# A hybrid sparse-attention block on one core: the softmax gate as a per-partition scalar, and the relu of the index scores left in PSUM

## The chip, the core and the metric

The kernel runs on 1 core of one Trainium2 chip. The metric is the device time of one execution in microseconds (us); before the change the median of 3 runs is 802.14 us (801.01 to 804.88). Lower is better.

## What is computed

One decoder block for 512 tokens of width 1024, in float32: a pre-norm, one wide input projection, two attention branches (A and B), sigmoid gates that merge them, an output projection, and a squared-relu MLP. The change touches two places, which the reference states so:

```python
# branch A: an index score picks 128 of the 512 keys for each query
s_h = jnp.einsum('bqhd,bsd->bqhs', qi, k_i).astype(jnp.float32)      # 8 index heads
score = jnp.einsum('bqh,bqhs->bqs', wi, jax.nn.relu(s_h))            # weighted sum of relus
...
# branch B: softmax over the selected keys (s), over a window (w) and over compressed keys (c)
gates = jax.nn.sigmoid(gates.astype(jnp.float32)).reshape(B, S, 3, G, R)
o = (gb[:, :, 0, :, :, None] * o_c + gb[:, :, 1, :, :, None] * o_s
     + gb[:, :, 2, :, :, None] * o_w)
```

A softmax row is `e / sum(e)`; the gate of a query and a head is one number per query, so the kernel multiplies it into `1 / sum(e)` before that factor is applied to the row.

## The kernel before

Tokens lie on the 128 partitions in four blocks j = 0 to 3, and all matmuls of weight and activation are split into a high and a low part, which makes three matmuls of one. The program has these stages: norm and first projections (to about 75 us), the attention stage (75 to about 375 us), the merge and output projection, the MLP (from about 460 us).

The attention stage is a list of 96 **units**, one per head, kind (`s` and `w` of branch B, then `a` of branch A) and block j. Unit j works on 128 queries and n = 128(j+1) keys. The 64 units of branch B come first (75 to about 290 us). A unit goes through `logits` (PE, into a PSUM tile of the tag `lg`, two buffers), `biased` (DVE, line 944: adds the bias strip, gives the negated logits `nl` and the row's minimum `nm`), `exps` (ACT, line 951: `pb` and the row sum `sm`), `recip` (DVE, lines 955 and 957), `norm` (ACT, line 964: `pb` times the factor `r`), `transposes` (PE, line 969) and `store` (ACT line 976, DVE line 977). The loop at line 1210 writes out the steps of three neighbouring units interleaved, and between them it takes matmuls from a list of other work ("filler": the remaining projections and the attention-times-value products) at a set pace. The order on PE is fixed by this loop; the order on DVE and ACT is made by a scheduler from the same program.

Beside the units run the **index scores** (`scores_job`, line 623) of the blocks j = 1, 2, 3. For each index head (for j = 1: for two heads at a time) PE writes the scores `sc` into a tile of the same tag `lg` (line 656), ACT takes the relu (line 647) into an SBUF tile `rl` of the tag `pb`, which has three buffers and is also that of `exps`, and DVE adds the relu times the head's weight `wi` to `work` in SBUF (line 651). The step of a head's relu and sum comes one step ahead of the next head's matmul, and in between the loop issues a unit's logits, so that the two buffers of `lg` go alternately to logits and to scores. There are 20 such relus and 24 sums. After them follow 16 rounds of max and match-replace per block (lines 669 and 670) on DVE.

POOL works at the same time, for the most part on the low parts of the weights: line 107 subtracts 128x1024 of SBUF from 128x1024 of SBUF.

The gate is a column of the SBUF tile `gates`, of 128x1; `r` and `sm` are SBUF tiles of 128x1 too:

```python
            self.r = r = t2.tile([P, 1], F32, tag="r", bufs=4, name="r" + self.name)
            V.reciprocal(r, self.sm)
            if self.gate is not None:
                V.tensor_mul(r, r, self.gate)
```

Of the kernel before, what the change touches and what calls it, by code (L numbers as in the profile page):

```python
# [15 lines left out]
F32 = mybir.dt.float32  # L16
F32R = mybir.dt.float32r
BF16 = mybir.dt.bfloat16
AF = mybir.ActivationFunctionType
ALU = mybir.AluOpType  # L20
AX = mybir.AxisListType

P = 128
# [42 lines left out]
def block_kernel(ctx, tc, x, norm_mix, w_in, pe_k, w1_k, w2_k, pe_v, w1_v, w2_v, rel_bias,  # L66
# [3 lines left out]
    V, A, G = nc.vector, nc.scalar, nc.gpsimd  # L70
# [3 lines left out]
    def pool(stack, name, side):  # L74
        return stack.enter_context(tc.tile_pool(name=name, bufs=1, side=side, reuse_waits="tile"))
# [9 lines left out]
    def ps(tag, name):  # L85
        return pp.tile([P, 512], F32, tag=tag, name=name)
# [438 lines left out]
    for dst, one, h, n in ((vr, onr, slice(0, 16), 320), (vf, onf, slice(8, 16), 504)):  # L525
        for n0 in range(0, dst.shape[1], n):
            o = ps("lg", f"vb{n}_{n0}")[:h.stop - h.start, :n]
# [31 lines left out]
    for j in range(NT):  # L559
        o = ps("mm" if j % 2 else "ov", f"ptok{j}")[:, :352]  # L560
# [14 lines left out]
    t2 = pool(t2s, "t2", "right")  # L575
# [47 lines left out]
    def scores_job(j):  # L623
        n = P * (j + 1)

        def run():
            if not works:
                works[0] = t2.tile([P, 1152], F32, tag="stm", name="work")
            work = works[0][:, sel_off[j]:sel_off[j] + n]
            ld(work, c_mask[:, 512 - n:])  # L630
            while len(qdone) < 2 or not kdone:
                yield
                yield
            Ui = cp.tile([P, 8, P], F32R, tag="Ui", bufs=1, name=f"Ui{j}")
            for c in range(4):
                nc.gpsimd.dma_start(Ui[32 * c:32 * c + 32],
                                    d_qi[c % 2].rearrange("(h d) t -> d h t", d=32)[:, :, j * P:(j + 1) * P])
            yield
            yield
            yield  # L640
            yield
            hn = 2 if j == 1 else 1
            o = None
            for h in range(0, 8 + hn, hn):
                if o is not None:
                    rl = t2.tile([P, 512], F32, tag="pb", bufs=3, name=f"rl{j}_{h}")
                    A.activation(rl[:, :hn * n], o[:, :hn * n], AF.Relu)
                    for i in range(hn):
                        g = h - hn + i
                        ri = rl[:, i * n:i * n + n]  # L650
                        V.scalar_tensor_tensor(work, ri, wi[:, j, g:g + 1], work, op0=ALU.mult, op1=ALU.add)  # L651
                yield
                if h < 8:
                    o = ps("lg", f"sc{j}_{h}")
                    for i in range(hn):
                        PE.matmul(o[:, i * n:i * n + n], Ui[:, h + i], KKi[:, :n], start=True, stop=True)
                    yield
            works[j] = work
            topk.append(top_k(j))

        return run
# [3 lines left out]
    def top_k(j):  # L665
        work, n = works[j], P * (j + 1)
        for r in range(16):
            m8 = t2.tile([P, 8], F32, tag="m8", bufs=4, name=f"m8_{j}_{r}")
            tc.keep_in_program_order(V.max(m8, work))  # L669
            V.match_replace(work, m8, work, -3.0e38)  # L670
            if r == 15:
                V.tensor_scalar(sel[:, sel_off[j]:sel_off[j] + n], work, -2.0e38, NEG, op0=ALU.is_gt, op1=ALU.mult)
            yield
# [252 lines left out]
    class Unit:  # L926
# [26 lines left out]
        def recip(self):  # L953
            self.r = r = t2.tile([P, 1], F32, tag="r", bufs=4, name="r" + self.name)
            V.reciprocal(r, self.sm)
            if self.gate is not None:
                V.tensor_mul(r, r, self.gate)  # L957

        def norm(self):
            pb = self.pb[:, :self.n]  # L960
# [466 lines left out]
    for half in range(2):  # L1427
        cs = slice(half * S, (half + 1) * S)
        wh, wl = wo[half]
        for j in range(NT):  # L1430
            js = slice(j * P, (j + 1) * P)
            o = ps("ov" if j % 2 else "lg", f"wo{half}{j}")
# [166 lines left out]
```

## Time and profile before

| what | value |
|---|---|
| median of 3 runs | 802.14 us (801.01 to 804.88) |
| the profiled execution | 804.47 us, of which the span of the trace is 802.6 us |
| PE busy | 759.7 us (95%) |
| DVE busy | 633.6 us (79%) |
| ACT busy | 442.6 us (55%) |
| POOL busy | 293.9 us (37%) |
| DMA | 95.54 MB moved, 119 GB/s in the mean |

A share of busy time is a mean over stages. What a change is worth must be read from the stage that it touches, and there from the waits that end last. A timeline row gives start, duration, engine, line, operation and tiles; in brackets stands how long the engine sat idle before it, and what ended that. Rows of DVE overlap a little, since the next instruction starts while the one before it drains.

### The profile page before, as it was taken

To read this page: it belongs to the slowest core of one execution; us is meant where nothing else is said; L and a number is where in the kernel's file an instruction comes from. 1 tells how busy PE (TensorE), PEld (TensorE's weight loads), DVE (VectorE), ACT (ScalarE), POOL (GpSimd) and SP (SyncE) were. 2 spreads that over 40 slices of the span, in tenths; PEclk is the share of its full clock that TensorE was granted. 3 is DMA by queue.
4 is the path that set the end of the run, shared out by engine and by line. 5 is a ranking of instruction groups with operands and counts; after the bars stand their busy time and mean duration, and the time that the engine had idled before them with its cause. 6 is when DMAs were issued, how large, how long until landed. Compare 5 with 4: busy or idle time off the path is not lost.

```text
span 802.6 us, 12188 instructions
## 1 busy us (share of the span) xinstructions
PE 759.7 (95%) x4267; PEld 650.2 (81%) x4267; DVE 633.6 (79%) x1354; ACT 442.6 (55%) x926; POOL 293.9 (37%) x178
## 2 busy tenths in 40 slices
PE   7999899998998899899989999989999999999997
PEld 4888687776886788777868989888989798989885
DVE  5344789999999977886866999986978879696734
ACT  6534786777667777784354655452617263444314
POOL 3714542322332347663160653330605042424022
PEclk9999999999999999999999999999999999999999
DMA  9554736342345335373740532250414141412002
GB/s 269 135 177 142 186 94 168 89 132 68 84 133 148 95 92 164 124 240 123 262 143 1 161 129 62 69 186 1 163 49 158 53 158 53 157 54 84 23 26 105
DMA packets 87501, 95.54 MB, mean 119 GB/s; under 512 B 8598, under 2 KB 69654, under 8 KB 87408
## 3 DMA queue, kind: packets, MB, share of 16 engines
q1 hardware_dynamic: 83984, 92.97, 37.3%
q0 software_dynamic: 3456, 1.80, 1.4%
q8 instruction: 34, 0.56, 0.3%
q14 instruction: 27, 0.22, 0.1%
HBM read 86.29 MB, written 14.74 MB: 126 GB/s over the span
## 4 chain that ended last, share of the span: by engine, by line
PE 54%; DVE 32%; DMA 5%; ACT 4%; issue 3%; POOL 1%; SPq 0%; DVEq 0%; ACTq 0%; POOLq 0%
PE mo L1550 6%; PE mo L1551 6%; PE mo L1549 6%; PE z L114 5%; PE z L118 5%; PE z L115 5%; PE wo L1441 3%; DVE work L670 3%; DVE m L669 3%; DVE ws L1333 2%; DVE work L651 2%; DVE rw L957 2%; DMA wmi<-in_w_mlp_in 2%; DVE wm L1337 2%; DVE nlw L944 1%
## 5 line engine op out<-in xcount | busy, mean ns | idle before, releaser
L1550 PE MATMUL mo<-wmol,ah 128*128 128x512 f32 (+1 forms) x260 | 101.9, 392 | 0.0
L1551 PE MATMUL mo<-wmoh,al 128*128 128x512 f32 (+1 forms) x260 | 101.1, 391 | 0.0
L1501 POOL TENSOR_TENSOR wmol<-wmor,wmoh 128x1024 fp32r<-128x1024 f32 x16 | 42.6, 2664 | 158.3 <-ACT wmoh L1500 132.9
L1549 PE MATMUL mo<-wmoh,ah 128*128 128x512 f32 (+1 forms) x260 | 100.4, 390 | 0.1
L1337 POOL TENSOR_TENSOR wm<-wmi,wm 128x512 fp32r<-128x512 f32 x32 | 60.2, 1896 | 64.8 <-ACT wm L1336 29.9
L1552 DVE SCALAR_TENSOR_TENSOR x<-mo,r,x 128x512 f32<-128x512 f32 (+1 forms) x65 | 47.5, 735 | 42.4 <-PE mo L1551 42.4
L1500 ACT CAST wmoh<-wmor 128x1024 fp32r<-128x1024 f32 x32 | 32.1, 1048 | 83.8 <-PE mo L1551 76.1
L1336 ACT CAST wm<-ws 128x512 fp32r<-128x512 f32 x80 | 48.0, 622 | 53.8 <-DVE ws L1333 35.0
L107 POOL TENSOR_TENSOR wg_l<-wr_g,wg_h 128x1024 fp32r<-128x1024 f32 x16 | 38.6, 2413 | 86.6 <-ACT pbs L964 23.0
L114 PE MATMUL z<-xshh,wm 128*128 128x256 f32 x256 | 65.0, 285 | 2.5 <-DVE zt L1353 2.5
L115 PE MATMUL z<-xshl,wm 128*128 128x256 f32 x256 | 64.9, 285 | 0.0
L1333 DVE TENSOR_TENSOR ws<-wmi 128x512 f32<-128x512 f32 x74 | 62.1, 847 | 0.5 <-DMA wmi<-in_w_mlp_in 0.5
L1337 DVE TENSOR_TENSOR wm<-ws,wm 128x512 fp32r<-128x512 f32 x70 | 54.6, 792 | 6.2 <-ACT wm L1336 6.2
L1549 PEld LDWEIGHTS mo<-wmoh,ah 128*128 128x128 f32 x260 | 49.0, 189 | 10.8 <-ACT ah L1490 0.3
L1551 PEld LDWEIGHTS mo<-wmoh,al 128*128 128x128 f32 x260 | 48.9, 189 | 10.5
L1550 PEld LDWEIGHTS mo<-wmol,ah 128*128 128x128 f32 x260 | 48.8, 188 | 10.4
L124 PE MATMUL pg<-hTh,wg_h 128*128 128x512 f32 x128 | 52.2, 408 | 0.0
L126 PE MATMUL pg<-hTl,wg_h 128*128 128x512 f32 x128 | 51.9, 406 | 0.0
L114 PEld LDWEIGHTS z<-xshh,wm 128*128 128x128 f32 x256 | 49.2, 192 | 3.3 <-issue 2.6
L1353 DVE TENSOR_TENSOR zt<-zt,z 128x256 f32<-128x256 f32 x128 | 47.8, 407 | 4.3 <-PE z L118 2.2
L115 PEld LDWEIGHTS z<-xshl,wm 128*128 128x128 f32 x256 | 49.2, 192 | 0.4
L118 PE MATMUL z<-xshh,wm 128*128 128x256 f32 x256 | 42.7, 285 | 0.0
(428 smaller groups left out, 2230.2 us busy)
## 6 DMA issues: line engine op xcount, KB each, us to landing
wmi<-in_w_mlp_in SPq DMA_DIRECT2D x32, 512.0 KB, 4.9
wmor<-in_w_mlp_out SPq DMA_DIRECT2D x32, 512.0 KB, 3.6
wr_g<-in_w_in SPq DMA_DIRECT2D x16, 512.0 KB, 3.9
d_rev<-d_vr SPq DMA_DIRECT2D x8, 640.0 KB, 6.0
x<-in_x SPq DMA_DIRECT2D x8, 512.0 KB, 8.4
d_t<-th SPq DMA_DIRECT2D x16, 256.0 KB, 2.1
stb<-d_rev SPq DMA_DIRECT2D x8, 256.0 KB, 2.9
wr_qa<-in_w_in SPq DMA_DIRECT2D x4, 512.0 KB, 4.1
```

Source lines behind the costliest of these rows:

```text
L114: PE.matmul(o, wh(k), xh(k), start=start and n == 0, stop=False)
L115: PE.matmul(o, wh(k), xl(k), start=False, stop=False)
L118: PE.matmul(o, wl(k), xh(k), start=False, stop=stop and k == nk - 1)
L124: PE.matmul(o, wh(k), xh(k), start=k == 0, stop=False)
L126: PE.matmul(o, wh(k), xl(k), start=False, stop=False)
L1333: V.tensor_tensor(t, src, more[0], op=w_blocks[m][2])
L1336: A.copy(w[:, 0], src)
L1337: (V if p > 1 and m in LOV else G).tensor_sub(w[:, 1], src, w[:, 0].bitcast(F32))
L1353: V.tensor_tensor(c, c, o, op=ALU.add if sign > 0 else ALU.subtract)
L1549: PE.matmul(o, act[f][0][:, js], wm[f][0][:, cs], start=f == 0, stop=False)
L1550: PE.matmul(o, act[f][0][:, js], wm[f][1][:, cs], start=False, stop=False)
L1551: PE.matmul(o, act[f][1][:, js], wm[f][0][:, cs], start=False, stop=f == FG - 1)
```

## The change

The gate multiply of the 64 units of branch B becomes a `tensor_scalar` whose factor is the gate's column as a per-partition scalar, in place of a `tensor_tensor` of two 128x1 tiles. The relu of the index scores is written over its own input in PSUM, the SBUF tile `rl` goes, and line 651 reads its relu from PSUM.

```diff
@@ -643,11 +643,10 @@
             for h in range(0, 8 + hn, hn):
                 if o is not None:
-                    rl = t2.tile([P, 512], F32, tag="pb", bufs=3, name=f"rl{j}_{h}")
-                    A.activation(rl[:, :hn * n], o[:, :hn * n], AF.Relu)
+                    A.activation(o[:, :hn * n], o[:, :hn * n], AF.Relu)
                     for i in range(hn):
                         g = h - hn + i
-                        ri = rl[:, i * n:i * n + n]
+                        ri = o[:, i * n:i * n + n]
                         V.scalar_tensor_tensor(work, ri, wi[:, j, g:g + 1], work, op0=ALU.mult, op1=ALU.add)
@@ -954,7 +953,7 @@
             V.reciprocal(r, self.sm)
             if self.gate is not None:
-                V.tensor_mul(r, r, self.gate)
+                V.tensor_scalar(r, r, self.gate, None, op0=ALU.mult)
```

The number of instructions on each engine stays the same. The order on PE, POOL and SP is the same in both programs; that of DVE and ACT is made anew by the scheduler. Lines behind 646 have one less in the changed program. Two places show what moved.

The first is DVE near the end of head 0's window units. `rw0_2` is the softmax factor of the unit of block 2, `nlw0_3` the biased logits of block 3, the rest belongs to the compressed keys. Before:

```order
L955 RECIPROCAL rw0_2_1003<-smw0_2_992 128x1
L957 TENSOR_TENSOR rw0_2_1003<-rw0_2_1003,gates_74 128x1
L944 ISA nlw0_3_1016,nmw0_3_1017<-lgw0_3_1013,stb0_768 128x512
L944 ISA nmw0_3_1017 128x1
L785 COPY ztk_1050<-ztk_1023 128x64
L797 CAST w2hk_1052<-w2rk_632 128x128
```

And in the changed program:

```order
L954 RECIPROCAL rw0_2_1003<-smw0_2_992 128x1
L943 ISA nlw0_3_1016,nmw0_3_1017<-lgw0_3_1013,stb0_768 128x512
L943 ISA nmw0_3_1017 128x1
L784 COPY ztk_1050<-ztk_1023 128x64
L796 CAST w2hk_1052<-w2rk_632 128x128
L956 TENSOR_SCALAR rw0_2_1003<-rw0_2_1003,gates_74 128x1
```

The gate multiply of this unit went behind the next unit's biased logits and two small instructions.

The second is DVE in the index scores of block 1 (`work` is the score, `rl` the relu in SBUF, `sc` the score tile in PSUM, `PTs` the stored softmax rows). Before:

```order
L651 SCALAR_TENSOR_TENSOR work_634<-rl1_6_1250,wi_76,work_634 128x256
L955 RECIPROCAL rw1_0_1269<-smw1_0_1255 128x1
L944 ISA nlw1_1_1298,nmw1_1_1299<-lgw1_1_1295,stb1_1069 128x256
L944 ISA nmw1_1_1299 128x1
L977 TENSOR_TENSOR PTs1_1177<-ts1_2_1263,PTs1_1177 128x3x128
L957 TENSOR_TENSOR rw1_0_1269<-rw1_0_1269,gates_74 128x1
```

And in the changed program:

```order
L650 SCALAR_TENSOR_TENSOR work_634<-sc1_4_1231,wi_76,work_634 128x256
L954 RECIPROCAL rw1_0_1266<-smw1_0_1252 128x1
L976 TENSOR_TENSOR PTs1_1176<-ts1_2_1260,PTs1_1176 128x3x128
L956 TENSOR_SCALAR rw1_0_1266<-rw1_0_1266,gates_74 128x1
L943 ISA nlw1_1_1295,nmw1_1_1296<-lgw1_1_1292,stb1_1069 128x256
L943 ISA nmw1_1_1296 128x1
```

The sum keeps its place and reads the score tile itself; here the gate multiply went ahead of the next unit's biased logits.

## Rows read from the trace of the kernel before

**Rows 1.** The page: the span

```profile
span 802.6 us, 12188 instructions
```

**Rows 2.** Busy us of each engine by stretch (the heading line names the columns)

```profile
core 0: us, PE busy (x) PEld busy (x) DVE busy (x) ACT busy (x) POOL busy (x), PEclk, DMA share, GB/s
75.00:107.00 32.00, 28.85 (x143) 23.78 (x143) 21.94 (x69) 23.75 (x56) 15.09 (x12) 0.95 0.65 164
107.00:203.00 96.00, 88.32 (x457) 71.76 (x457) 92.37 (x278) 70.30 (x159) 31.65 (x20) 0.98 0.43 116
203.00:292.00 89.00, 82.67 (x439) 67.79 (x438) 85.53 (x267) 63.92 (x152) 27.08 (x16) 1.00 0.39 116
```

**Rows 3.** The chain that ended last, 75 to 292 us, by engine and line

```profile
by line: DVE work L670 10.3%; DVE m L669 9.5%; DVE work L651 6.3%; DVE rw L957 6.1%; DVE nlw L944 5.4%; DVE PTs L977 5.3%; DVE nls L944 4.7%; DMA w1rv<-in_cmp_w_v 4.2%; DVE rs L957 4.0%; DVE PTw L977 3.8%; issue 3.1%; DVE opb L1010 2.1%; PE
```

**Rows 4.** Waits of PE, 75 to 292 us: total us, times, longest

```profile
PE tw L969 <- ACT pbw L964: 5.3, 7, 1.7
...
PE ts L969 <- ACT pbs L964: 2.3, 4, 0.9
PE ob L997 <- DVE PTw L977: 2.2, 1, 2.2
```

**Rows 5.** Groups of DVE by form: busy us, mean ns, idle before

```profile
L1552 DVE SCALAR_TENSOR_TENSOR x<-mo,r,x 128x512 f32<-128x512 f32 x63 | 46.6, 744 | 42.4 <-PE mo L1551 42.4
...
L957 DVE TENSOR_TENSOR rw<-rw,gates 128x1 f32<-128x1 f32 x32 | 15.7, 491 | 0.2
L957 DVE TENSOR_TENSOR rs<-rs,gates 128x1 f32<-128x1 f32 x32 | 15.5, 486 | 0.4
...
L651 DVE SCALAR_TENSOR_TENSOR work<-rl,wi,work 128x512 f32<-128x512 f32 x8 | 7.9, 992 | 0.6 <-ACT rl L647 0.6
...
L651 DVE SCALAR_TENSOR_TENSOR work<-rl,wi,work 128x384 f32<-128x384 f32 x8 | 5.7, 714 | 0.0
```

**Rows 6.** Line 957 alone: duration in ns, least, median, most

```profile
L957 DVE TENSOR_TENSOR rs<-rs,gates x32: 134/156/2089, 76.1 to 281.7; 128x1 f32<-128x1 f32 x32
```

**Rows 7.** Timeline of POOL and DVE from 110.37 us

```profile
110.37 2.40 POOL L107 TENSOR_TENSOR wqb_l<-wr_qb,wqb_h 128x1024 fp32r<-128x1024 f32 x1 [4.44 <-issue]
...
110.78 0.16 DVE L955 RECIPROCAL rs<-sms 128x1 f32<-128x1 f32 x1 [1.03 <-ACT pbs L951]
...
110.98 1.80 DVE L957 TENSOR_TENSOR rs<-rs,gates 128x1 f32<-128x1 f32 x1
```

**Rows 8.** Timeline of POOL and DVE from 795.44 us, in the last norm

```profile
795.44 1.98 POOL L1523 TENSOR_TENSOR y<-x,gfin 128x512 f32<-128x512 f32 x2 [3.14 <-DVE x L1552]
...
796.15 0.15 DVE L1522 TENSOR_SCALAR fss<-fss 128x1 f32<-128x1 f32 x1 [0.40 <-ACT fsq L1519]
...
796.56 0.21 DVE L1522 TENSOR_SCALAR fss<-fss,fss 128x1 f32<-128x1 f32 x1 [0.25 <-ACT fsq L1519]
```

**Rows 9.** Line 890, a tensor_scalar of 8 elements: least, median, most ns

```profile
L890 DVE TENSOR_SCALAR cm<-cm x4: 152/168/2197, 158.2 to 233.8; 128x8 f32<-128x8 f32 x4
```

**Rows 10.** Timeline from 186.07 and from 253.01 us: long DVE rows, PE's waits behind

```profile
186.07 2.73 DVE L651 SCALAR_TENSOR_TENSOR work<-rl,wi,work 128x512 f32<-128x512 f32 x1
...
194.34 0.76 PE L1037 MATMUL oc<-PTc,VVc 128*128 128x512 f32 x1 [3.19 <-DVE tmp L1012]
...
253.01 2.09 DVE L957 TENSOR_TENSOR rs<-rs,gates 128x1 f32<-128x1 f32 x1
...
256.24 0.51 PE L997 MATMUL ob<-PTw,VV 128*128 128x512 f32 x1 [2.24 <-DVE PTw L977]
```

**Rows 11.** Timeline of the scores: a matmul, and the sum of the head before

```profile
154.89 0.44 PE L656 MATMUL sc<-KKi,Ui 128*128 128x384 f32 x1
...
155.93 0.61 DVE L651 SCALAR_TENSOR_TENSOR work<-rl,wi,work 128x384 f32<-128x384 f32 x1
...
171.62 0.75 DVE L651 SCALAR_TENSOR_TENSOR work<-rl,wi,work 128x512 f32<-128x512 f32 x1
...
172.93 0.39 PE L656 MATMUL sc<-KKi,Ui 128*128 128x512 f32 x1
```

## The prediction

> **What bounds the kernel now.** I read the busy time by stretch first, then the chain, PE's waits, and last the timeline around the rows that the change touches. The span is 802.6 us [rows 1] of a profiled execution of 804.47 us. The change touches only branch B's units and the index scores, and both lie between 75 and 292 us. There PE is busy for 28.85 + 88.32 + 82.67 = 199.8 of 217 us, so it idles for 17.2 us; DVE is busy for 96% of the time from 107 us on (92.37 of 96, 85.53 of 89) [rows 2]. PE's order is fixed, so nothing that DVE does can save more here than PE's idle time and what its clock lost; the granted clock is 0.95 and 0.98 in the first two stretches, so for a part of them PE ran at 1.2 in place of 2.4 GHz [rows 2]. The chain of this stage runs mostly over DVE, and the gate multiply of line 957 holds 6.1% + 4.0% of it, 21.9 us, for an instruction on one element per partition [rows 3].
>
> The reason stands in the groups by form. The 64 gate multiplies take 15.7 + 15.5 = 31.2 us, 0.49 us each [rows 5], while the median of one kind is 0.156 and the longest 2.089 us [rows 6]. At the median they would take 64 x 0.156 = 10.0 us, so 21.2 us are stall. The timeline shows on what: POOL starts a subtract of two SBUF tiles at 110.37 us and ends at 112.77; in that time the reciprocal, with one input, takes 0.16 us, and the multiply behind it, with two inputs in SBUF, starts at 110.98 and ends at 112.78, when POOL does [rows 7]. POOL is busy for a third of the stage [rows 2], so a multiply meets it often. Line 651 shows the same, with `rl` and `work` both in SBUF: one sum of 512 columns takes 2.73 us at 186.07 [rows 10], the mean is 0.992, and line 1552, of the same form but with one tensor in PSUM, takes 0.744 [rows 5].
>
> **The gate multiply, 64 times.** The new form has one tensor input and a scalar per partition. Two rows have it at 128x1, both in the last norm: 0.15 us with a constant factor and 0.21 us with a factor per partition, while POOL works from 795.44 to 797.42 on two SBUF tiles; the first starts well inside that and is over at 796.30 [rows 8]. I take 0.21 us: 64 x 0.21 = 13.4 us, a saving of 17.8 us on DVE. The ends are 0.15 us each, a saving of 21.6 us, and the old stalls with 0.06 us more each, a loss of 3.8 us. Against the better end speaks a tensor_scalar of 8 elements per partition: the least takes 0.152 and the most 2.197 us [rows 9], so this operation too can stall when it is wider. [...]
>
> **The relu and the 24 sums.** The relu itself stays on ACT with as many elements. The sums lose their second SBUF input: 8 x (0.992 - 0.744) = 2.0 us, and 8 x (0.714 - 0.61) = 0.8 us for 384 columns, with 0.61 from an undisturbed one [rows 5, 11]; those of 256 columns showed no excess. The relus also leave the three buffers of `pb`, which can only help `exps`; I count nothing.
>
> **A new wait.** The tile in PSUM is now free only when DVE has read it, not when ACT has. The next head's matmul takes the same buffer, since logits and scores alternate on two. In the trace one matmul starts at 154.89 us while the sum of the head before ends at 156.54, 1.65 us later; another starts at 172.93 with its sum done at 172.37 [rows 11]. There are 3 + 7 + 7 = 17 such pairs in the three blocks, so the bounds are nothing and 28 us. Much of the lag is the backlog that the gate's stalls make on DVE, and PE waits for DVE at the next logits in any case. I take 0.12 us a pair, 2.0 us; this is the term I trust least.
>
> **The new order.** Gate multiplies move both ways against their neighbours, as the two listed places show, one behind and one ahead of a `biased` of 0.5 to 0.7 us; I count nothing.
>
> **The sum, on PE.** 1. Transposes that wait for `norm` (5.3 + 2.3 = 7.6 us [rows 4]): `norm` needs the gate multiply, but other things come late too; half, 3.8 us. 2. The wait for the stored rows behind the multiply of 253.01 us: 2.2 us [rows 4, 10]. 3. The wait of 3.19 us at 194.34, behind the sum of 186.07: that sum's excess, 2.73 - 0.74 = 2.0 us [rows 10]. 4. The rest of PE's idle time, 17.2 - 7.6 - 2.2 - 3.2 = 4.2 us, mostly backlog of DVE: half, 2.1 us. 5. Clock: 0.05 x 32 + 0.02 x 96 = 3.5 us were lost [rows 2]; with shorter idle stretches 1.4 come back. 6. The slower multiply where nothing stalled, 64 x 0.06 = 3.8 us on DVE, nearly all behind PE's work: -0.5. 7. The new wait: -2.0. Together 9.0 us. Against the profiled execution that is 795.5 us; that execution lies 2.3 us above the median of 802.14, and runs of the changed kernel compare with the median, so I forecast 793.1 us. DVE would then be some 20 us less busy over the stage, and PE its bound; nothing behind 292 us should change but its start.
>
> **Rivals.**
> - *The new multiply stalls as the old one* (for it: rows 9; against: rows 8). Terms 1, 2 and 5 go, and half of 4; what is left is 2.0 + 1.0 - 0.5 - 2.0 = 0.5 us, so 801.6 us. This is also the case in which the change doesn't do what it says. [...]
> - *The new wait decides.* PE's score matmul waits for the sum, and every filler matmul behind it in PE's fixed order waits too. Without term 7 the gains are 11.0 us; at 0.65 us a pair (17 x 0.65) they are gone, and from 0.9 us a pair the kernel is slower by over 0.5%. At 1.0 us, two thirds of the late pair, it is 802.14 - 11.0 + 17.0 = 808.1 us. For it speaks the late pair, against it that DVE loses its stalls of up to 2 us just ahead of these sums.
> - *The stalls move on.* POOL is as busy as before, and the next DVE instruction with two inputs in SBUF meets it in the multiply's place. If half of the stalled time comes back, terms 1 to 5 (11.5 us) halve to 5.8 and with -2.5 give 3.3 us: 798.8 us. Against it: most DVE instructions of the stage read PSUM or one tensor.
> - *All of PE's idle time goes*, with most of the clock: 17.2 us, about 785 us. Against it: a chain of four engines per unit keeps some waits.
>
> **How the numbers follow.** Forecast (788 to 798 us) 0.58; multiply still stalls 0.12; new wait 0.10; stalls move 0.08; larger gain 0.12. A measurement of this kernel tells about 0.5% from no change (its three runs span that much), so faster is below 798.1 us and slower above 806.2. Faster 0.58 + 0.12 = 0.70, within 0.5% 0.12 + 0.08 = 0.20, slower 0.10. The range reaches from the larger gain to the stalled multiply with a little of the new wait's upper bound: 784 to 803 us, with the new wait left out.
>
> **What would show it.** Right: line 957's successor at 0.15 to 0.25 us with no row near 2 us, also under POOL; line 651's successor at about 0.74 us for 512 columns; PE's idle time from 75 us to the end of branch B near 9 us; the first unit of branch A some 9 us earlier and the same distance kept to the end. Wrong: rows of 1 to 2 us in the gate multiply (first rival); waits of PE's `sc` matmul for line 651's successor of over 0.65 us each (second); long rows in lines 891, 901, 902 or 1013 in their place (third).

## The result, and the profile after

Before: 801.68 us in the median of 7 runs (798.09 to 804.88). After: 795.76 us in the median of 7 runs (793.62 to 799.22). The ratio is 0.993, with a 95% interval of 0.9902 to 0.9957, so the kernel is faster by 0.4 to 1.0%. The profiled execution of the changed kernel took 794.45 us; its page says of the span and of VectorE:

```profile
span 792.6 us, 12175 instructions
...
PE 755.1 (95%) x4267; PEld 648.3 (82%) x4267; DVE 623.4 (79%) x1354; ACT 442.3 (56%) x926; POOL 293.5 (37%) x178
```

The two profiled executions are 10.0 us apart, the medians 5.9 us: the one of before lay 2.8 us above its median, the one of after 1.3 us below. DVE is 10.2 us less busy. Line numbers behind 646 are one less than before.

The gate multiply and the sums, as groups of DVE by form in the changed kernel (busy us, mean ns, idle before), against [rows 5]:

```profile
L956 DVE TENSOR_SCALAR rs<-rs,gates 128x1 f32<-128x1 f32 x32 | 6.6, 207 | 0.3
L956 DVE TENSOR_SCALAR rw<-rw,gates 128x1 f32<-128x1 f32 x32 | 6.5, 204 | 0.2
...
L650 DVE SCALAR_TENSOR_TENSOR work<-sc,wi,work 128x512 f32<-128x512 f32 x8 | 5.9, 739 | 0.0
...
L898 DVE TENSOR_SCALAR cs<-cs 128x8 f32<-128x8 f32 x4 | 4.9, 1226 | 0.0
L650 DVE SCALAR_TENSOR_TENSOR work<-sc,wi,work 128x384 f32<-128x384 f32 x8 | 4.9, 610 | 0.0
...
L848 DVE TENSOR_TENSOR VVc<-vs,rowm 128x512 fp32r<-128x512 f32 x2 | 3.1, 1552 | 0.0
...
L759 DVE TENSOR_TENSOR zv<-hv 64x128 f32<-64x128 f32 x1 | 2.3, 2319 | 0.0
...
L765 DVE TENSOR_SCALAR uv<-uv 64x128 f32<-64x128 f32 x1 | 1.8, 1847 | 0.0
...
L759 DVE TENSOR_TENSOR zk<-hk 64x128 f32<-64x128 f32 x1 | 1.6, 1598 | 0.0
```

The first two lines are the 64 gate multiplies: 13.1 us in place of 31.2. Lines 898, 848, 759 and 765 are where stall has appeared (`zk`, `zv`, `uk` and `uv` are tiles of the gelu in the two networks that make branch B's compressed keys and values, `VVc` and `cs` come behind it; PE's transposes `ztk` and `ztv` below take the gelu's result): before, `zv` and `zk` took 0.27 and 0.29 us, this `uv` 0.22, the mean of `VVc` was 0.68 and of `cs` 0.79. How even the new multiply is shows in its own view (duration in ns: least, median, most), against [rows 6]:

```profile
L956 DVE TENSOR_SCALAR rs<-rs,gates x32: 185/206/216, 76.2 to 269.1; 128x1 f32<-128x1 f32 x32
L956 DVE TENSOR_SCALAR rw<-rw,gates x32: 190/204/215, 87.7 to 277.9; 128x1 f32<-128x1 f32 x32
```

Of the 64, 14 began while POOL worked on a subtract with at least 0.1 us to go, and none of them took over 0.216 us; before, 18 began so, and 17 of them took 0.28 to 2.34 us.

The timeline of POOL and DVE in the changed kernel shows which instruction now meets POOL (start, us, engine, line):

```profile
114.78 2.42 POOL L107 TENSOR_TENSOR wqb_l<-wr_qb,wqb_h 128x1024 fp32r<-128x1024 f32 x1
120.97 2.35 POOL L107 TENSOR_TENSOR wg_l<-wr_g,wg_h 128x1024 fp32r<-128x1024 f32 x1 [3.77 <-ACT uv L769]
...
115.04 2.32 DVE L759 TENSOR_TENSOR zv<-hv 64x128 f32<-64x128 f32 x1
...
121.43 0.21 DVE L956 TENSOR_SCALAR rw<-rw,gates 128x1 f32<-128x1 f32 x1
121.55 1.85 DVE L765 TENSOR_SCALAR uv<-uv 64x128 f32<-64x128 f32 x1
```

At 121.43 the gate multiply runs through POOL's subtract undisturbed; the next instruction, a scale of 64x128 from SBUF to SBUF, waits for POOL's end (123.32). At 115.04 it is a sum of two halves in SBUF.

Busy time by stretch, against [rows 2], and PE's waits from 75 to 285 us (total us, times, longest), against [rows 4]:

```profile
core 0: us, PE busy (x) PEld busy (x) DVE busy (x) ACT busy (x) POOL busy (x), PEclk, DMA share, GB/s
75.00:107.00 32.00, 30.89 (x167) 25.98 (x167) 24.27 (x78) 27.46 (x64) 15.88 (x13) 1.00 0.76 181
107.00:203.00 96.00, 89.04 (x470) 73.12 (x469) 91.49 (x292) 72.85 (x167) 33.57 (x22) 1.00 0.43 119
203.00:285.00 82.00, 79.75 (x427) 66.51 (x426) 74.55 (x247) 60.54 (x144) 25.47 (x14) 1.00 0.40 124
```

```profile
PE ztv L781 <- DVE zv L766: 2.5, 1, 2.5
PE ts L968 <- ACT pbs L963: 2.1, 3, 0.8
PE tw L968 <- ACT pbw L963: 1.6, 2, 0.9
PE oc L1036 <- DVE tmp L1011: 1.3, 2, 1.1
PE ztk L781 <- DVE zk L766: 1.1, 1, 1.1
PE sc L655 <- DVE nmw L943: 0.6, 1, 0.6
PE lgw L936 <- DVE rw L954: 0.5, 1, 0.5
PE lgw L936 <- DVE work L650: 0.5, 1, 0.5
```

PE idles for 10.3 us (210 - 30.89 - 89.04 - 79.75) in place of 17.2, at a granted clock of 1.00 throughout. The first logits of branch A start here; before, it was at 288.4 us:

```profile
L936 PE MATMUL lga<-kah,ua x32: 274/308/397, 276.9 to 351.6; 128*128 128x128 f32 x8, 128*128 128x256 f32 x8, 128*128 128x384 f32 x8, 128*128 128x512 f32 x8
```

So in these two executions the stage, from branch B's first logits (74.7 us in both) to branch A's, went from 213.7 to 202.2 us, by 11.5. From there to the MLP's first matmul it took 2.0 us more (160.0 us before, 162.0 after); PE's waits of `ta` for DVE's `pba` (branch A's transposes and softmax rows) were 3.5 us before and 4.9 after.

### The profile page after: what moved, and what is told of

The parts are those of the page before. It is cut to its first block, busy times and chain, and to the rows that moved or that the text cites. A ratio compares the mean times of both kernels' runs of the same rounds, so it can differ in the third digit from the quotient of the medians.

```text
span 792.6 us, 12175 instructions
## 1 busy us (share of the span) xinstructions
PE 755.1 (95%) x4267; PEld 648.3 (82%) x4267; DVE 623.4 (79%) x1354; ACT 442.3 (56%) x926; POOL 293.5 (37%) x178
## 4 chain that ended last, share of the span: by engine, by line
PE 57%; DVE 27%; ACT 6%; DMA 5%; issue 3%; POOL 1%; SPq 0%; DVEq 0%; ACTq 0%; POOLq 0%
PE mo L1549 6%; PE mo L1550 6%; PE mo L1548 6%; PE z L114 5%; PE z L115 5%; PE z L118 5%; PE wo L1440 3%; DVE ws L1332 2%; DVE work L669 2%; DVE m L668 2%; PE pg L126 2%; PE pg L124 2%; DVE wm L1336 2%; DMA wmi<-in_w_mlp_in 2%; PE pg L129 1%
## 5 line engine op out<-in xcount | busy, mean ns | idle before, releaser
L1500 POOL TENSOR_TENSOR wmol<-wmor,wmoh 128x1024 fp32r<-128x1024 f32 x16 | 42.6, 2665 | 157.9 <-ACT wmoh L1499 132.5
```

## The experiments

Each ratio is against runs of the kernel before on the same chip, whose medians were 800.26 to 801.36 us. "The stage" is the time just defined.

**The changed kernel once more.** No edit beside the change.

> The changed kernel again, on the same chip as its parts. Theory (the gate multiply no longer waits for POOL, the rest of the change is small): 0.5% to 1% faster than before, about 4 to 8 us. If the first comparison was luck of the runs: within 0.3% of before.

Measured: 794.0 us, ratio 0.9922 (0.9893 to 0.995). The result stands. Its profile differs from the first in places: PE idles for 12.9 us from 75 to 285 us, with a granted clock of 0.95 in the first stretch. Two executions of one program thus differ by 2.6 us of idle time and, at 0.05 x 32, 1.6 us of clock in this stage alone. Here the stage takes 206.3 us (73.0 to 279.3) and the way from there to the MLP 158.9 us, with 3.4 us of waits of `ta` for `pba`. So the 202.2 and the 162.0 us of the first execution are good to some 4 and 3 us, and only differences well over that can be read from a single execution. PE's longest waits in the stage are these; in the first execution of the changed kernel `ztk` waited 1.1 us:

```profile
PE ztk L781 <- DVE zk L766: 3.7, 1, 3.7
PE ztv L781 <- DVE zv L766: 2.5, 1, 2.5
```

**The gate alone.**

```diff
-                V.tensor_mul(r, r, self.gate)
+                V.tensor_scalar(r, r, self.gate, None, op0=ALU.mult)
```

> The gate multiply as a per-partition scalar alone; the relu still goes to SBUF. Theory: nearly all of the gain, 4 to 7 us faster than before; the multiply's 64 rows fall from 31.2 to about 13 us, and line 651, with two SBUF inputs, now meets POOL more often: 17.4 us of busy time rise to 18 to 24. Rival (the relu carries the gain, by the freed buffers of pb or by the sums): within 1.5 us of before.

Measured: 796.07 us, ratio 0.9945 (0.9927 to 0.9963). Groups of DVE by form, with the relu still in SBUF:

```profile
L651 DVE SCALAR_TENSOR_TENSOR work<-rl,wi,work 128x384 f32<-128x384 f32 x8 | 8.3, 1035 | 0.0
L651 DVE SCALAR_TENSOR_TENSOR work<-rl,wi,work 128x512 f32<-128x512 f32 x8 | 8.1, 1014 | 0.0
L651 DVE SCALAR_TENSOR_TENSOR work<-rl,wi,work 128x256 f32<-128x256 f32 x8 | 7.8, 974 | 0.0
```

The sums, with both tensors in SBUF, took over stalls: 24.2 us in place of 17.4. The gate multiplies are as short as in the whole change (185 to 216 ns), and this part alone gives 0.55% of the 0.7 to 0.8%, so most of the gain is theirs.

**The relu alone.** The diff of the change without its last hunk.

> The relu in PSUM alone; the gate multiply is a tensor_tensor as before. Theory: within 2 us of before, line 651 at about 14.6 us, the gate multiply still at 28 to 36 us. Rival (the new wait of PE's score matmul for the sum costs something that the gate's part hides in the whole change): 2 to 8 us slower than before, with PE waits at the score matmul of over 5 us. Rival (the relu carries the gain): 4 us faster or more.

Measured: 799.64 us, ratio 0.999 (0.997 to 1.001): nothing that can be told from no change. The sums fall to 14.6 us, but the gate multiply keeps its stalls, by its own view:

```profile
L956 DVE TENSOR_TENSOR rs<-rs,gates x32: 133/156/2154, 74.7 to 280.7; 128x1 f32<-128x1 f32 x32
L956 DVE TENSOR_TENSOR rw<-rw,gates x32: 137/150/2816, 86.7 to 288.6; 128x1 f32<-128x1 f32 x32
```

PE's waits for a PSUM tile of logits or scores rise to 2.4 + 1.5 + 1.2 + 0.5 = 5.6 us, from 2.3 in the kernel before (1.6 in the whole change). The longest, in the timeline of DVE and PE:

```profile
111.48 2.15 DVE L956 TENSOR_TENSOR rs<-rs,gates 128x1 f32<-128x1 f32 x1
113.56 0.47 DVE L650 SCALAR_TENSOR_TENSOR work<-sc,wi,work 128x256 f32<-128x256 f32 x1
...
114.55 0.47 DVE L650 SCALAR_TENSOR_TENSOR work<-sc,wi,work 128x256 f32<-128x256 f32 x1
114.94 0.14 DVE L954 RECIPROCAL rw<-smw 128x1 f32<-128x1 f32 x1
...
115.16 0.36 PE L936 MATMUL lgw<-kwh,ub 128*128 128x256 f32 x1 [2.40 <-DVE rw L954]
```

A gate multiply waits for POOL, two sums wait behind it, and the logits start once both have read the score tile (the row names the reciprocal beside the second sum). So the new wait is longer while the gate stalls, in this one execution; the median shows no loss by it. The parts alone give 0.55% and 0.1%, together 0.7 to 0.8%; with these intervals that is no more than a sum.

**A factor two elements wide.** The new multiply, on a tile of 128x2 whose second column nobody reads:

```diff
-            self.r = r = t2.tile([P, 1], F32, tag="r", bufs=4, name="r" + self.name)
-            V.reciprocal(r, self.sm)
-            if self.gate is not None:
-                V.tensor_scalar(r, r, self.gate, None, op0=ALU.mult)
+            two = t2.tile([P, 2], F32, tag="r", bufs=4, name="r" + self.name)
+            self.r = r = two[:, 0:1]
+            if self.gate is None:
+                V.reciprocal(r, self.sm)
+            else:
+                V.reciprocal(two, self.sm.to_broadcast([P, 2]))
+                V.tensor_scalar(two, two, self.gate, None, op0=ALU.mult)
```

> As the whole change, but the softmax factor and its gate multiply are two equal elements per partition wide instead of one. Theory (a tensor_scalar between SBUF tiles waits for POOL from two elements on, as the rows of 8 elements did): the multiply's 64 rows go back to 25 to 35 us with rows of up to 2.4 us, and the time back to within 3 us of before. Rival (it is the missing second input alone that frees the multiply, whatever the width): rows of 0.2 us and the time of the whole change.

Measured: 800.71 us, ratio 1.0012 (0.9987 to 1.0036). The whole gain is gone. The multiply's own view:

```profile
L959 DVE TENSOR_SCALAR rs<-rs,gates 128x2 f32<-128x2 f32 x32 | 19.2, 600 | 0.3
L959 DVE TENSOR_SCALAR rw<-rw,gates 128x2 f32<-128x2 f32 x32 | 16.0, 501 | 0.2
```

The undisturbed duration hardly differs (medians of 228 and 221 ns), the longest is 2.82 us. The reciprocal, two elements wide too, takes 0.15 us in the mean as in the whole change. All 17 that began inside a subtract of POOL took 0.36 to 2.26 us. So the missing second tensor alone does not keep the new multiply clear of POOL: with two elements the same operation waits, with one it doesn't.

**POOL's subtracts replaced by fills.** In the kernel before, and in the changed one, lines 107 and 729 fill the low parts with zeros; the low parts of these weights are left out of the computation.

```diff
-        G.tensor_sub(lo, src, hi.bitcast(F32))
+        G.memset(lo.bitcast(F32), 0.0)
...
-                            G.tensor_sub(t[:, :, 1], r, t[:, :, 0].bitcast(F32))
+                            G.memset(t[:, :, 1].bitcast(F32), 0.0)
```

> The kernel before, with POOL's weight subtracts in the attention stage (the low parts in split_w and in halves) replaced by POOL memsets of zero over the same tiles: the low parts of those weights are left out of the computation. POOL then writes as many elements but reads none. Theory (the gate multiply waits for POOL's reads of SBUF): the 64 multiplies, unchanged, fall from 31.2 us to under 14 us, and the time falls by 6 to 14 us. Rival (any work of POOL makes them wait, writes too): 20 us or more, with rows of 1 to 2 us.

> The changed kernel with the same POOL memsets in place of the subtracts, so with the same part left out. Theory (the change is worth only what it takes from the waits for POOL): no gain is left over the kernel before with memsets; within 2 us of it, on the slow side by some 60 ns a multiply and the wait for the score tile, if anything. Rival (the change also gains by its order or by the freed buffers): 4 us or more faster than that one.

Measured: 776.44 us without the change (0.9675 to 0.9738) and 779.97 with it (0.9707 to 0.9766). The first kernel's group of the fill on POOL, and the old gate multiply's own view:

```profile
L107 POOL MEMSET wg_l<- 128x1024 f32 x16 | 15.3, 955 | 92.1 <-PE pg L129 46.8 <-PE pqa L129 15.8 <-PE pqb L129 13.7
```

```profile
L957 DVE TENSOR_TENSOR rs<-rs,gates x32: 135/153/748, 73.2 to 256.6; 128x1 f32<-128x1 f32 x32
L957 DVE TENSOR_TENSOR rw<-rw,gates x32: 136/150/660, 83.4 to 264.4; 128x1 f32<-128x1 f32 x32
```

The old multiplies sum to 11.0 us and the stage takes 191.6 us (71.8 to 263.4), with the change 194.0. The longest old multiplies, of 0.75, 0.66 and 0.35 us, did not wait for a fill: each ran beside one of the subtracts of POOL that this edit leaves (lines 1066 and 1127), and ended with it. The 8 that began inside a fill took 0.15 to 0.16 us. In the changed kernel one multiply took 0.95 us beside a fill; the instruction ahead of it on DVE, a tensor_scalar of eight elements, stood there as long, and both ended with the fill (149.52). The timelines of POOL and DVE, first without the change, then with it:

```profile
253.42 1.29 POOL L1066 TENSOR_TENSOR obl<-opb,obh 128x512 fp32r<-128x512 f32 x1
253.98 0.75 DVE L957 TENSOR_TENSOR rs<-rs,gates 128x1 f32<-128x1 f32 x1
```

```profile
148.53 1.00 POOL L107 MEMSET wqa_l<- 128x1024 f32 x1
148.54 1.02 DVE L889 TENSOR_SCALAR cm<-cm 128x8 f32<-128x8 f32 x1
148.61 0.95 DVE L956 TENSOR_SCALAR rw<-rw,gates 128x1 f32<-128x1 f32 x1
```

So two-input multiplies wait where POOL subtracts and not where it fills. Where POOL doesn't hold DVE up, the change gains nothing; it is 3.5 us slower between the medians of four runs each, with intervals that overlap. Of the 22.1 us by which the stage is shorter with the fills (213.7 - 191.6), the change brings back 11.5 in its first execution and 7.5 in its second. This is a bound and no clean price: a fill takes 0.96 us where the subtract took 2.41, and it needn't wait for ACT's high part.

**The gelu out of POOL's way.** The sums that took over the stalls, with operands in PSUM and the square on ACT:

```diff
-                V.tensor_add(t, t, h1[0:64, :256])
-                V.tensor_add(z, t[:, 0:P], t[:, P:])
-                V.tensor_mul(u, z, z)
+                V.tensor_add(z, t[:, 0:P], u)
+                V.tensor_add(w, t[:, P:], w)
+                V.tensor_add(z, z, w)
+                A.activation(u, z, AF.Square)
```

(`u` and `w` are here the two halves of `h1` in PSUM.)

> The changed kernel, with the gelu of the two compression networks taken off the two-input reads of SBUF too: its sum of halves and its cubic polynomial are kept in the PSUM tile of the hidden layer, one square goes to ACT. In the changed kernel its rows met POOL in the multiply's place, and PE waited 1.1 to 3.7 and 2.5 us for it. Theory: these two waits shrink to under 1 us each and the time falls by 1 to 4 us against the changed kernel, so 7 to 11 us against before. Rival (the stalls move on once more, or the PSUM tile held longer delays a projection): within 1 us of the changed kernel or slower.

Measured: 795.52 us, ratio 0.9936 (0.9915 to 0.9958), no better than the change. The waits of `ztk` and `ztv` are gone, but PE has a new one:

```profile
PE pqb L124 <- DVE zk L767: 5.8, 1, 5.8
```

The PSUM tile, kept until the gelu ends, is the one that a projection waits for. It is a wait of the kind that the prediction feared for the relu.

**POOL's subtract in four pieces.** Nothing is left out; the work is the same.

```diff
-        G.tensor_sub(lo, src, hi.bitcast(F32))
+        n = shape[1] // 4
+        for i in range(0, shape[1], n):
+            G.tensor_sub(lo[:, i:i + n], src[:, i:i + n], hi[:, i:i + n].bitcast(F32))
```

> The kernel before, with GpSimd's subtract of line 107 (128x1024, 2.40 us each) written as four pieces of 128x256 (the kernel before has other subtracts of that shape at 0.68 us). Nothing is left out. Theory (a VectorE instruction that stands against a GpSimd instruction waits until that one instruction ends, and then gets in): no gate multiply of line 957 is longer than some 0.8 us, its 64 rows sum to 14 to 22 us in place of 31.2, and the kernel is 4 to 10 us faster than before, that is 790 to 796. Rival (GpSimd's next piece takes the memory back at once, so that the stalls have the same sum, or the four fixed costs make the weights late): multiplies of 2 us stay or TensorE waits for weights, and the time is within 1.5 us of before.

> The changed kernel with the same four pieces. Theory: the sums of gelu and the softmax scale, which took over about 8 us of the stalls, lose them; 2 to 7 us faster than the changed kernel, 8 to 14 us faster than before (786 to 793), and 0 to 5 us faster than the kernel before with the pieces, since the gate and the relu still save the time of short stalls. Rival: within 1.5 us of the changed kernel (794 to 797).

Measured: 790.88 us on the kernel before (ratio 0.9873, 0.9842 to 0.9904) and 789.79 with the change (0.9863, 0.9833 to 0.9893). On the kernel before, the gate multiplies fell from 31.2 to 18.9 us, and the stage to 203.0 us (74.2 to 277.2), about what the change gives it (202.2 and 206.3). One of the 64 contradicts the expectation that none is longer than 0.8 us, in the timeline of POOL and DVE:

```profile
86.77 2.81 POOL L109 TENSOR_TENSOR wg_l<-wr_g,wg_h 128x256 fp32r<-128x256 f32 x4
...
86.51 3.49 DVE L959 TENSOR_TENSOR rw<-rw,gates 128x1 f32<-128x1 f32 x1
```

It waited through all four pieces; of the other 63 none is longer than 0.70 us. So a waiting instruction of DVE mostly gets in between two pieces, but not always. This is no accident of one execution: in the later run with all pieces on the kernel before, the same multiply takes 3.63 us at the same place (85.28), and one row of `cm`, a tensor_scalar of eight elements, waits through three or four pieces (2.2 to 2.6 us) in every run with pieces. Why these are not let in was not tried. With the change, the stage takes 202.4 us (74.7 to 277.1), and `uk` (3.04 us) and `zv` (1.74 us) still wait, and PE's `ztk` and `ztv` behind them for 2.9 and 1.3 us. That part of the expectation fell. By the medians the pieces gain 4 to 6 us on the changed kernel; where is not shown. Against its first execution the gain lies behind the stage (158.5 us from branch A's first logits to the MLP, in place of 162.0), against its second in the stage (206.3 and 158.9 us).

**All of POOL's subtracts for weights in pieces of 256 columns.** The changed kernel with the last edit, the two halves of line 729, and in the MLP:

```diff
-        (V if p > 1 and m in LOV else G).tensor_sub(w[:, 1], src, w[:, 0].bitcast(F32))
+        if p > 1 and m in LOV:
+            V.tensor_sub(w[:, 1], src, w[:, 0].bitcast(F32))
+        else:
+            for k in range(0, 4, 2):
+                G.tensor_sub(w[:, 1, k:k + 2], src[:, k:k + 2], w[:, 0, k:k + 2].bitcast(F32))
...
-        (V if ff % 4 in LOO else G).tensor_sub(lo, r, hi.bitcast(F32))
+        if ff % 4 in LOO:
+            V.tensor_sub(lo, r, hi.bitcast(F32))
+        else:
+            for c in range(0, DM, 256):
+                G.tensor_sub(lo[:, c:c + 256], r[:, c:c + 256], hi[:, c:c + 256].bitcast(F32))
```

> The changed kernel with these pieces, and with GpSimd's other subtracts for weights cut too (the halves of line 729 and the expert layers' weights in two, the output weights in four). Theory: VectorE's rows of about 2 us in the expert layers shrink as well; 0 to 6 us faster than the changed kernel with the first pieces alone. Rival: in the expert layers TensorE or the transfers set the time and not VectorE, so within 1.5 us of it, or slower by the added fixed costs of some 0.1 us a piece where GpSimd is late.

Measured: 781.55 us, ratio 0.9763 (0.9731 to 0.9795). That beats both kernels, by some 19 and 12 to 14 us; the 8.2 us against the run before are more than the expected 0 to 6. The MLP's own DVE subtracts of the output weights, in the changed kernel and then here, as groups by form:

```profile
L1500 DVE TENSOR_TENSOR wmol<-wmor,wmoh 128x1024 fp32r<-128x1024 f32 x16 | 33.3, 2078 | 6.2 <-ACT wmoh L1499 6.1
```

```profile
L1508 DVE TENSOR_TENSOR wmol<-wmor,wmoh 128x1024 fp32r<-128x1024 f32 x16 | 23.0, 1439 | 6.2 <-ACT wmoh L1506 6.1
```

POOL pays for it: the pieces of the same weights take 64.7 us there, against 42.6 us whole. All that PE waits for a piece of POOL behind 285 us is 0.6 us. The MLP, from its first to its last matmul, goes from 347.5 to 343.7 us.

**The pieces with and without the change.** All pieces on the kernel before, and the last kernel again beside it.

> The kernel before with all the pieces of the last run (all of GpSimd's subtracts for weights in pieces 256 wide), without the gate as a scalar and without the relu in PSUM. Theory (the change is worth only what it takes from waits for GpSimd, and cutting those subtracts takes nearly all of it away): 780 to 785, within 3 us of the changed kernel with all pieces (781.55). Rival (the gate and the relu save the vector engine some time of their own beside the waits): 785 to 789, 4 to 7 us slower than the changed kernel with all pieces, as the change alone brought.

> The changed kernel with all pieces once more, on the same chip as the run beside it: 780 to 783.

Measured: 783.91 us without the change (0.9761 to 0.9814) and 782.58 with it (0.973 to 0.9784). The intervals overlap: with short POOL instructions, the 1.3 us between the medians can't be told from nothing. The old gate multiplies cost 19.7 us here, the new ones 13.1.

## Why the prediction was right

**The forecast.** 793.1 us stood against 795.76, inside the likeliest case's own 788 to 798, and "faster by over 0.5%" came true at 0.7%, and at 0.8% in the second comparison, though the first interval reaches down to 0.4%. The gain was smaller than the 9.0 us forecast: 5.9 and 6.7 us between the medians.

**The gate multiply.** Forecast 13.4 us for 64 of them, measured 13.1; no row is longer than 0.216 us. Taking the nearest row [rows 8] rather than the wider one [rows 9] was right, and the run with two elements shows why both rows were true. The Trainium skill's page "VectorE: DVE Perf Modes", section on mode 2×_2P, asks for an outermost non-unit dimension that is even, or odd and equal in source and destination. The traces agree: two elements fulfil that, and all 17 multiplies that began inside a subtract waited; one element has no non-unit dimension, and none of the 14 that began so waited.

**The sums.** Forecast -2.8 us; measured 8 x (0.992 - 0.739) + 8 x (0.714 - 0.610) = 2.8 us. What they are worth in time is not shown: alone the relu gives nothing to be measured, and the intervals of the gate alone and of the whole change overlap. That the gate alone pushes 6.8 us of stall into these sums was not in the prediction.

**The new wait.** Forecast 2.0 us. In the profile 0.5 us of `lgw` are put down to the sum and 0.5 to a reciprocal that ran beside one: 1.0 us. All waits for tiles of this tag fell from 2.3 to 1.6 us. The reason given, that the lag was mostly the gate's backlog, fits: with the gate's stalls in place they are 5.6. What was wrong is that each of the 17 pairs shares a buffer: here one score matmul starts at 143.08 us while the sum of the head before starts at 144.02, and the logits at 144.68 wait in its place.

**The sum on PE.** Term 1, transposes: 7.6 to 3.7 us, so 3.9 against 3.8. Term 2, the stored rows: gone, as forecast. Term 3: 3.2 to 1.3 us, 1.9 against 2.0. Term 5, the clock (its 1.4 us came from no row): granted 1.00 in all three stretches, 3.5 us, but only the 1.9 us from 107 to 203 us were there in the second execution too. That the first execution's own sum, 6.9 us of idle time and 3.5 of clock, comes near the forecast is thus in part luck: the clock and the new wait came out better than taken, term 4 worse. In the second execution the same sum is 4.3 + 1.9 = 6.2 us.

**The step that failed** is term 4, half of the other 4.2 us of idle time. Without the waits of terms 1 and 3 and the new one, 10.3 - 3.7 - 1.3 - 1.0 = 4.3 us are idle after, as 4.2 were before, and 3.6 of them are new: `ztv` and `ztk`, behind gelu's sums, which now meet POOL (6.2 us in the second execution). This is the third rival, in part. It had 0.08 with the argument that most DVE instructions of the stage read PSUM or one tensor. By line, DVE saved 18.1 + 2.8 = 20.9 us in the two places of the change, and 8.4 us came back: 3.4 in line 759, 1.6 in 765, 1.8 in 848, 1.7 in 898, 0.9 in 762, less 0.5 each in two others. The prediction looked for them in lines 891, 901, 902 and 1013; the costly ones stood in the gelu, ahead of a PE matmul. DVE was therefore not 20 us less busy but 10 over the program, and from 107 to 203 us it still is for 95%, more than PE (93%), so PE didn't become the bound there.

**The way from the profile to the median.** The 9.0 us were taken off the median whole. The profile of before was 2.8 us above the median, and two executions of one program differ in this stage's idle time and clock by some 4 us, so a part of what was read as idle was that one execution's. Which part was not separated. Branch A began 11.5 us earlier in the first execution and 9.1 in the second, against the 9 forecast. Whether that distance is kept to the end can't be told: the way on to the MLP was 2.0 us longer than before in the first execution and 1.1 us shorter in the second.

**The other rivals.** That the multiply stalls as before: not so, but at two elements it is what happens, down to the time (800.71 us against the 801.6 worked out). That the new wait decides: not for the relu, but in the gelu experiment such a wait took 5.8 us. That all idle time goes: only without POOL's subtracts.

## What to carry to other kernels

When a tiny VectorE instruction shows a median of 0.15 us and a maximum of 2, look at what GpSimd runs at that moment; taking one waiting instruction out lets the next one of that kind wait, so count all of them in the stage before crediting the stall. Here the better remedy stood on the other side: GpSimd's long instructions in pieces gave as much in the stage as the change did, helped the rest of the program too, and with all of them in pieces the kernel took 781.6 us; the medians with and without the change were then only 1.3 us apart. A tile held in PSUM to spare VectorE a second SBUF operand is paid for by whoever needs that tile next, 1.0 us in one place and 5.8 in another.

## What was not expected of the hardware

- A tensor_scalar from SBUF to SBUF passed POOL's subtracts untouched with one element per partition (185 to 216 ns in 128 of 128 rows of the changed kernel and of the gate alone), and waited for them with two (up to 2818 ns).
- The old multiply of 128x1 waits up to 2.8 us behind a POOL subtract that reads two tensors; the 8 that began inside POOL's fills of the same tiles took 0.15 to 0.16 us. The Trainium skill, page "SBUF — State Buffer", section "Who interferes with whom", says that a VectorE instruction with two SBUF inputs contends with a GpSimd instruction that reads SBUF, not with one that only writes it. The traces agree. A tensor_scalar of eight elements did wait for a fill (1.02 us in one row).
- The same section calls the port pair that VectorE and GpSimd share an exclusive lock. In pieces of 0.7 us, 63 of 64 multiplies waited no longer than one piece; one waited 3.49 us, through four in a row, and did so again (3.63 us) in another run with pieces.
- Cutting a 128x1024 subtract of POOL into four, beside a busy DVE, took POOL 64.7 us in place of 42.6 for the same 16 weights, in a run in which the program was shorter all the same.
